# Hardware loops on ScalarE and VectorE in a batched A·Bᵀ kernel, with GpSimd passing on DMA landings as counts

## The chip, the cores and the metric

One core of one Trainium2 chip. The metric is the device time of one execution in microseconds (us). The span of a profile, from first to last instruction, is some 1.8 us shorter than the timed run (124.3 against 126.1 us for the profiled run of before). A run counts as slow when it is over 1.5% above the fastest of the same kernel. The granted clock is the share of TensorE's full clock that the profile records as granted.

## The reference

```python
a: (16, 512, 512) float32      # batch, m, k
b: (16, 512, 512) float32      # batch, n, k
out = np.matmul(a, b.transpose(0, 2, 1)).astype(np.float32)
```

33.55 MB are read and 16.78 MB written.

## The kernel before

Two batch entries form a pair; there are eight. Tiles of 2 MB are loaded into seven buffers. VectorE casts them to bf16 (first half of k into h, second half into w, later copied w to h). TensorE (PE) transposes them into PSUM; VectorE evicts (copies out of PSUM) the transposes of b into tb, ScalarE those of a into ta. PE multiplies, ScalarE evicts the products into one of seven output buffers. PE runs a hardware loop over pairs already; ScalarE and VectorE are unrolled. Their parts, cut:

```python
for u in range(pairs):                                  # VectorE, unrolled in Python
    for x, (h, w, s_c, s_t) in enumerate(both):         # both = a's and b's buffers
        n = 2 * u + x
        src = ld[n % NL]                                # a constant slot
        nc.vector.wait_ge(s_ld[n % NL], 16 * (n // NL + 1))    # the DMA's own semaphore
        ...                                             # n < 2: in two halves, as each lands
        nc.vector.tensor_copy(out=h[:], in_=src[:, :, :HK]).then_inc(s_c, 1)
        nc.vector.tensor_copy(out=w[:], in_=src[:, :, HK:]).then_inc(s_cd, 1)
    for ko in range(KO): ...                            # ha<-wa, tb0, hb<-wb, tb1, tb2, tb3

nc.scalar.nop().then_inc(s_ea, 2)
for u in range(pairs):                                  # ScalarE, unrolled in Python
    for ko in range(KO):
        nc.scalar.wait_ge(s_ta, KO * u + ko + 1)
        ...                                             # two copies ta<-tp
    for e in range(2):
        i = 2 * u + e
        ...                                             # wait for the store of i - NO
        for j in range(J):
            nc.scalar.wait_ge(s_mm, J * i + j + 1)
            ...                                         # copy ob[i % NO]<-ps[j]; s_pv or s_out
```

Of the kernel before, what the change touches and what calls it, by code (L numbers as in the profile page):

```python
# [10 lines left out]
def kernel(  # L11
# [6 lines left out]
    nc = tc.nc  # L18
    P = 128
    batch, M, K = a.shape  # L20
    _, N, _ = b.shape
    J = M // P
    KO = K // P
    HP = P // 2
    HK = K // 2
    pairs = batch // 2
    f32 = mybir.dt.float32
    bf16 = mybir.dt.bfloat16
    NL = 7
    NO = 7  # L30


    ORDER = "LLLLLLLSLLLLSLSSLSLSLLSSSSSSSSS"

    def sbuf(name, shape, dtype):
        return ctx.enter_context(nc.sbuf_tensor(name, shape, dtype))

    def sem(name):
        return tc.alloc_semaphore(name)

    with tc.tile_critical(no_gpsimd_drain=True):  # L41
        ident = sbuf("ident", [P, P], bf16)
        ld = [sbuf(f"ld{i}", [P, 2 * J, K], f32) for i in range(NL)]
        ha, wa, hb, wb = (
            sbuf(name, [P, 2 * J, HK], bf16) for name in ("ha", "wa", "hb", "wb")
        )
        ta = sbuf("ta", [P, KO, 2 * J * P], bf16)
        tb = sbuf("tb", [P, KO, 2 * J * P], bf16)
        ob = [sbuf(f"ob{i}", [P, J, N], f32) for i in range(NO)]
        tp = ctx.enter_context(nc.psum_tensor("tp", [P, 4, 2 * J, P], bf16))  # L50
        ps = ctx.enter_context(nc.psum_tensor("ps", [P, 4, N], f32))

# [1 line left out]
        s_ld = [sem(f"s_ld{i}") for i in range(NL)]  # L54
        s_second = [sem(f"s_second{i}") for i in range(2)]
        s_st = [sem(f"s_st{i}") for i in range(NO)]
        s_cd = sem("s_cd")
        s_ca = sem("s_ca")
        s_cb = sem("s_cb")
        s_ta = sem("s_ta")  # L60
        s_tb = sem("s_tb")
        s_ea = sem("s_ea")
        s_eb = sem("s_eb")
        s_mm = sem("s_mm")
        s_pv = sem("s_pv")
        s_out = sem("s_out")
# [5 lines left out]
            out=ident[:], in_=ident[:], compare_op=mybir.AluOpType.not_equal, fill=1.0,  # L72
# [4 lines left out]



        n_ld, n_st = 0, 1  # L80
        for what in ORDER:
            if what == "L":
                u, slot = n_ld // 2, n_ld % NL
                src = (a if n_ld % 2 == 0 else b)[2 * u:2 * u + 2].rearrange(
                    "e (p j) k -> (e p) j k", j=2 * J
                )
                if n_ld >= NL:

                    nc.sync.wait_ge(s_cd, n_ld - NL + 1)
                if n_ld < 2:  # L90
                    nc.sync.dma_start(
                        ld[slot][:, :J, :], src[:, :J, :]
                    ).then_inc(s_ld[slot], 16)
                    nc.sync.dma_start(
                        ld[slot][:, J:, :], src[:, J:, :]
                    ).then_inc(s_second[slot], 16)
                else:
                    nc.sync.dma_start(ld[slot][:], src).then_inc(s_ld[slot], 16)
                n_ld += 1
            else:  # L100
                slot = n_st % NO
                nc.sync.wait_ge(s_out, n_st + 1)
                nc.sync.dma_start(
                    out[n_st].rearrange("(p j) n -> p j n", j=J), ob[slot][:]
                ).then_inc(s_st[slot], 16)
                n_st += 1
        for n in range(batch - NO, batch - 1):
            nc.sync.wait_ge(s_st[n % NO], 16 * (n // NO + 1))




        nc.vector.nop().then_inc(s_eb, 2)
        nc.vector.wait_ge(s_set, 2)
        both = ((ha, wa, s_ca, s_ta), (hb, wb, s_cb, s_tb))
        for u in range(pairs):
            for x, (h, w, s_c, s_t) in enumerate(both):
                n = 2 * u + x
                src = ld[n % NL]
                nc.vector.wait_ge(s_ld[n % NL], 16 * (n // NL + 1))  # L120
                nc.vector.wait_ge(s_t, KO * u)
                if n >= 2:
                    nc.vector.tensor_copy(out=h[:], in_=src[:, :, :HK]).then_inc(s_c, 1)  # L123
                    nc.vector.tensor_copy(out=w[:], in_=src[:, :, HK:]).then_inc(s_cd, 1)  # L124
                else:
                    nc.vector.tensor_copy(out=h[:, :J, :], in_=src[:, :J, :HK])  # L126
                    nc.vector.tensor_copy(out=w[:, :J, :], in_=src[:, :J, HK:])  # L127
                    nc.vector.wait_ge(s_second[n], 16)
                    nc.vector.tensor_copy(  # L129
                        out=h[:, J:, :], in_=src[:, J:, :HK]  # L130
                    ).then_inc(s_c, 1)
                    nc.vector.tensor_copy(  # L132
                        out=w[:, J:, :], in_=src[:, J:, HK:]
                    ).then_inc(s_cd, 1)
            for ko in range(KO):
                if ko < 2:
                    h, w, s_c, s_t = both[ko]
                    nc.vector.wait_ge(s_cd, 2 * u + ko + 1)
                    nc.vector.wait_ge(s_t, KO * u + 2)
                    nc.vector.tensor_copy(out=h[:], in_=w[:]).then_inc(s_c, 1)  # L140
                nc.vector.wait_ge(s_tb, KO * u + ko + 1)
                nc.vector.tensor_copy(  # L142
                    out=tb[:, ko, :],
                    in_=tp[:, 2 + ko % 2].rearrange("k j p -> k (j p)"),
                ).then_inc(s_eb, 1)


        nc.scalar.nop().then_inc(s_ea, 2)
        for u in range(pairs):
            for ko in range(KO):  # L150

                nc.scalar.wait_ge(s_ta, KO * u + ko + 1)
                for e in range(2):
                    c = nc.scalar.copy(  # L154
                        out=ta[:, ko, e * J * P:(e + 1) * J * P].rearrange(
                            "k (j p h) -> k j p h", j=J, h=2
                        ),
                        in_=tp[:, ko % 2, :, e * HP:(e + 1) * HP].rearrange(
                            "k (h j) p -> k j p h", h=2
                        ),  # L160
                    )
                c.then_inc(s_ea, 1)
            for e in range(2):
                i = 2 * u + e
                if i >= NO:
                    nc.scalar.wait_ge(s_st[i % NO], 16 * (i // NO))
                for j in range(J):
                    nc.scalar.wait_ge(s_mm, J * i + j + 1)

                    c = nc.scalar.copy(  # L170
                        out=ob[i % NO][:, j, :].rearrange("m (p j) -> m p j", j=2 * J),
                        in_=ps[:, j, :].rearrange("m (j p) -> m p j", j=2 * J),
                    )
                    if j == J - 1:
                        c.then_inc(s_out, 1)
                    elif e == 0 or j == 0:
                        c.then_inc(s_pv, 1)
                    if i == 1 and j == 0:
                        nc.scalar.wait_ge(s_out, 1)
                        nc.scalar.dma_start(  # L180
                            out[0].rearrange("(p j) n -> p j n", j=J), ob[0][:]
                        ).then_inc(s_st[0], 16)


        def take(s, n):
            nc.tensor.wait_ge(s, n).then_inc(s, -n)  # L186

        pe = nc.tensor.engine
        with nc.Fori(0, pairs, engines=[pe]):
            with nc.Fori(0, 2, engines=[pe]):  # L190

                for x, (h, s_c, s_t, s_e) in enumerate(
                    ((ha, s_ca, s_ta, s_ea), (hb, s_cb, s_tb, s_eb))
                ):
                    take(s_c, 1)
                    for g in range(2):
                        take(s_e, 1)
                        for j in range(2 * J):
                            t = nc.tensor.transpose(  # L199
                                tp[:, 2 * x + g, j, :], h[:, j, g * P:(g + 1) * P], ident[:]  # L200
                            )
                        t.then_inc(s_t, 1)
            nc.tensor.wait_ge(s_ea, 2)
            nc.tensor.wait_ge(s_eb, 2)


            for e in range(2):
                for j in range(J):
                    if e == 1 and j % 2 == 0:
                        take(s_pv, 2)  # L210
                    for ko in range(KO):
                        t = nc.tensor.matmul(  # L212
                            ps[:, j, :],
                            ta[:, ko, (e * J + j) * P:(e * J + j + 1) * P],
                            tb[:, ko, :].rearrange("k (j p) -> k j p", j=2 * J)[
                                :, :, e * HP:(e + 1) * HP
                            ],
                            start=(ko == 0),
                            stop=(ko == KO - 1),
                        )  # L220
                    t.then_inc(s_mm, 1)
# [34 lines left out]
```

## Time and profile before

| | before |
|---|---|
| time, median of the first 3 runs | 127.23 us (127.03 to 127.98) |
| span of the profile | 124.3 us |
| DMA | 50.33 MB, engines over 90% busy in all slices but the ends |
| PE, VectorE, ScalarE busy | 74%, 55%, 57% |
| matmuls of one pair to those of the next | 12.40 to 12.46 us |
| last eviction done | 115.43 us |

### The profile page before, as it was taken

The numbers are of one execution on the slowest core, as the hardware profiler recorded it, in microseconds if no ns is written. First come the engines' busy times: TensorE is split into PE (matmuls) and PEld (weight loads), VectorE is DVE, ScalarE is ACT, GpSimd is POOL, SyncE is SP. The second block draws the span as 40 slices with busy tenths as digits, with TensorE's granted clock in tenths as the row PEclk, the third lists the DMA queues.
The fourth block names the chain that finished last, engine by engine and source line by source line (L and its number), as shares of the span: only waits on it lengthen the run. The fifth ranks groups of instructions, "written<-read, shape, count | busy, mean of one in ns | idle before, by whom it ended". The sixth has DMA issues, their size and how long they took to land. (4 is left out here: it accounts for less than half of the span.)

```text
span 124.3 us, 2076 instructions
## 1 busy us (share of the span) xinstructions
PE 91.8 (74%) x768; PEld 56.5 (45%) x768; DVE 67.9 (55%) x84; ACT 71.0 (57%) x129; POOL 0.7 (1%) x6
## 2 busy tenths in 40 slices
PE   0005397998699869986998699869986998699000
PEld 0005394447444744574447444744474447443000
DVE  0065668827891788278907890782686568400000
ACT  4006042769476946694669476947694769476100
POOL 2000000000000000000000000000000000000000
PEclk9999999999999999999999999999999999999955
DMA  3999999999999999999999999999999999999980
GB/s 79 403 427 451 443 427 427 427 427 374 411 427 424 445 432 443 424 422 430 414 430 406 416 451 387 403 451 416 448 427 422 419 422 427 427 427 427 424 377 34
DMA packets 4898, 50.35 MB, mean 405 GB/s; under 512 B 544, under 2 KB 544, under 8 KB 544
## 3 DMA queue, kind: packets, MB, share of 16 engines
q1 hardware_dynamic: 4752, 49.29, 94.5%
q10 hardware_dynamic: 144, 1.05, 2.0%
q14 instruction: 2, 0.02, 0.0%
HBM read 33.55 MB, written 16.78 MB: 405 GB/s over the span
## 5 line engine op out<-in xcount | busy, mean ns | idle before, releaser
L212 PE MATMUL ps<-tb,ta 128*128 128x512 bf16 x256 | 57.3, 379 | 8.0 <-DVE tb L142 8.0
L170 ACT COPY ob<-ps 128x512 f32<-128x512 f32 x64 | 37.6, 587 | 30.1 <-PE ps L212 30.1
L212 PEld LDWEIGHTS ps<-tb,ta 128*128 128x128 bf16 x256 | 23.9, 97 | 39.0 <-ACT ta L154 8.2
L154 ACT COPY ta<-tp 128x512 bf16<-128x512 bf16 x64 | 32.9, 604 | 13.3 <-PE tp L199 12.9
L199 PE MATMUL tp<-ident,ha 128*128 128x128 bf16 x256 | 19.7, 230 | 11.8 <-PEq L186 10.9
L199 PEld LDWEIGHTS tp<-ident,ha 128*128 128x128 bf16 x256 | 16.7, 104 | 15.5 <-issue 13.8
L142 DVE COPY tb<-tp 128x1024 bf16<-128x1024 bf16 x32 | 21.3, 685 | 3.9 <-PE tp L199 3.6
L199 PE MATMUL tp<-ident,hb 128*128 128x128 bf16 x256 | 18.5, 230 | 3.1 <-PEq L186 3.1
L199 PEld LDWEIGHTS tp<-ident,hb 128*128 128x128 bf16 x256 | 16.3, 104 | 3.4 <-issue 3.3
L140 DVE COPY ha<-wa 128x2048 bf16<-128x2048 bf16 x8 | 5.5, 693 | 18.1 <-PE tp L199 18.1
L123 DVE CAST hb<-ld 128x2048 bf16<-128x2048 f32 x7 | 8.6, 1226 | 7.2 <-DMA ld<-in_b_dram 7.2
L123 DVE CAST ha<-ld 128x2048 bf16<-128x2048 f32 x7 | 8.5, 1219 | 0.6 <-DMA ld<-in_a_dram 0.6
L124 DVE CAST wb<-ld 128x2048 bf16<-128x2048 f32 x7 | 8.5, 1221 | 0.0
L124 DVE CAST wa<-ld 128x2048 bf16<-128x2048 f32 x7 | 8.5, 1220 | 0.0
L140 DVE COPY hb<-wb 128x2048 bf16<-128x2048 bf16 x8 | 5.5, 685 | 0.2 <-PE tp L199 0.2
L126 DVE CAST ha<-ld 128x1024 bf16<-128x1024 f32 x1 | 0.7, 694 | 6.1 <-DMA ld<-in_a_dram 6.1
L154 ACT ACT_TABLE_LOAD x1 | 1.3, 1283 | 1.0 <-SPq L41 1.0
L129 DVE CAST hb<-ld 128x1024 bf16<-128x1024 f32 x1 | 0.7, 694 | 1.2 <-DMA ld<-in_b_dram 1.2
L126 DVE CAST hb<-ld 128x1024 bf16<-128x1024 f32 x1 | 0.7, 695 | 1.2 <-DMA ld<-in_b_dram 1.2
L129 DVE CAST ha<-ld 128x1024 bf16<-128x1024 f32 x1 | 0.7, 694 | 1.1 <-DMA ld<-in_a_dram 1.1
L132 DVE CAST wa<-ld 128x1024 bf16<-128x1024 f32 x1 | 0.7, 689 | 0.0
L127 DVE CAST wa<-ld 128x1024 bf16<-128x1024 f32 x1 | 0.7, 687 | 0.0
(8 smaller groups left out, 2.3 us busy)
## 6 DMA issues: line engine op xcount, KB each, us to landing
out_dram<-ob SPq DMA_DIRECT2D x15, 1024.0 KB, 25.8
ld<-in_a_dram SPq DMA_DIRECT2D x7, 2048.0 KB, 30.8
ld<-in_b_dram SPq DMA_DIRECT2D x7, 2048.0 KB, 30.5
ld<-in_a_dram SPq DMA_DIRECT2D x2, 1024.0 KB, 6.1
ld<-in_b_dram SPq DMA_DIRECT2D x2, 1024.0 KB, 10.1
out_dram<-ob ACTq DMA_DIRECT2D x1, 1024.0 KB, 12.2
```

The source lines that it names most:

```text
L123: nc.vector.tensor_copy(out=h[:], in_=src[:, :, :HK]).then_inc(s_c, 1)
L124: nc.vector.tensor_copy(out=w[:], in_=src[:, :, HK:]).then_inc(s_cd, 1)
L126: nc.vector.tensor_copy(out=h[:, :J, :], in_=src[:, :J, :HK])
L127: nc.vector.tensor_copy(out=w[:, :J, :], in_=src[:, :J, HK:])
L129: nc.vector.tensor_copy(out=h[:, J:, :], in_=src[:, J:, :HK]).then_inc(s_c, 1)
L132: nc.vector.tensor_copy(out=w[:, J:, :], in_=src[:, J:, HK:]).then_inc(s_cd, 1)
L140: nc.vector.tensor_copy(out=h[:], in_=w[:]).then_inc(s_c, 1)
L142: nc.vector.tensor_copy(out=tb[:, ko, :], in_=tp[:, 2 + ko % 2].rearrange("k j p -> k (j p)"),).then_inc(s_eb, 1)
L154: c = nc.scalar.copy(out=ta[:, ko, e * J * P:(e + 1) * J * P].rearrange("k (j p h) -> k j p h", j=J, h=2), in_=tp[:, ko % 2, :, e * HP:(e ...
L170: c = nc.scalar.copy(out=ob[i % NO][:, j, :].rearrange("m (p j) -> m p j", j=2 * J), in_=ps[:, j, :].rearrange("m (j p) -> m p j", j=2 * J),)
L199: t = nc.tensor.transpose(tp[:, 2 * x + g, j, :], h[:, j, g * P:(g + 1) * P], ident[:])
L212: t = nc.tensor.matmul(ps[:, j, :], ta[:, ko, (e * J + j) * P:(e * J + j + 1) * P], tb[:, ko, :].rearrange("k (j p) -> k j p", j=2 * J)[:, ...
```

## The change

The intent: less program. ScalarE and VectorE run one turn of a hardware loop per pair, with buffer slots held in registers. The waits of a loop body are written once, with one count and one semaphore for all turns, so each wait takes its counts back ("take": wait, then subtract), and GpSimd turns the DMAs' semaphores into one count for loads (s_go) and one for freed output buffers (s_of). All stores go out from the SyncE queue. Cut to its core:

```diff
-    ORDER = "LLLLLLLSLLLLSLSSLSLSLLSSSSSSSSS"
+    ORDER = "LLLLLLLSSLLLLSLSSLSLSLLSSSSSSSSS"
...
-                    nc.sync.wait_ge(s_cd, n_ld - NL + 1)
+                    nc.sync.wait_ge(s_cd, n_ld - NL + 2)
...
+                nc.gpsimd.wait_ge(s_ld[n_ld % NL], 16 * (n_ld // NL + 1)).then_inc(s_go, 1)
...
+        def taker(engine):
+            return lambda s, n: engine.wait_ge(s, n).then_inc(s, -n)
...
-        for u in range(pairs):
+        with nc.Fori(0, pairs, engines=[dve]) as u:
...
+                src = ld[:, bass.ds((u * 2 + x) % NL, 1)].rearrange("p o j k -> p (o j) k")
+                take(s_go, 1)
+                nc.vector.tensor_copy(out=h[:], in_=src[:, :, :HK]).then_inc(s_c, 1)
+                ...                                # w in two halves, s_cd on the first
...
         nc.scalar.nop().then_inc(s_ea, 2)
+        nc.scalar.nop().then_inc(s_of, NO)
-        for u in range(pairs):
+        with nc.Fori(0, pairs, engines=[act]) as u:
...
+            take(s_of, 2)
             for e in range(2):
+                dst = ob[:, bass.ds((u * 2 + e) % NO, 1)].rearrange("m o j n -> m (o j) n")
...
-                    if i == 1 and j == 0:          # the store of out 0 from ScalarE's queue
-                        ...
...
+                            if x == 1 and g == 0 and j == 0:     # PE: ha has been read
+                                t.then_inc(s_da, 1)
```

## The prediction

The forecast came to 127.1 us, with a range of 126.4 to 129.0.

- *The first pair and the second bound:* the time that GpSimd takes to pass a landing on, the author's estimate. The +0.8 us of the first pair contain it.
- *The slack:* the time from a DMA's issue to its first bytes. The average end of the transfers, the 118.5 us as the latest end of compute and so the "about 3 us" were worked out with it, as estimates. What before shows is 1.0 us (first load issued at 0.94 us, first packet at 1.95 us).
- *Rivals B and C*, with chances of 0.05 and 0.02: back edges that wait for an instruction fetch, and casts that get slower when their slot comes from a register.

Three measured facts of before: by the packets, the slowest of the 16 DMA engines was done at 122.5 us; the one store on ScalarE's queue took 2.0% of engine time for 1.05 MB, as much per MB as the SyncE queue's 94.5% for 49.29 MB; and the casts of 128x2048 took 1219 to 1226 ns, which the prediction assumed for the loop too.

> **What bounds the kernel now.** I read the page's slices first, then the table of stages, then the chain of waits, then the issues of the SyncE queue.
>
> ```profile
> DMA  3999999999999999999999999999999999999980
> ...
> HBM read 33.55 MB, written 16.78 MB: 405 GB/s over the span
> ...
> out_dram<-ob SPq DMA_DIRECT2D x15, 1024.0 KB, 25.8
> ld<-in_a_dram SPq DMA_DIRECT2D x7, 2048.0 KB, 30.8
> ```
>
> All slices but the first and the last have the DMA engines at 9 tenths or more, and a transfer takes 25 to 31 us from issue to landing although 1 MB at the slices' usual 427 GB/s needs only 2.5 us: it stands in a backlog. 50.33 MB / 427 GB/s = 117.9 us[...]. The span is 124.3 us. So DMA bandwidth sets the time, and compute matters only if it lets the backlog run dry.
>
> How near is compute to that? The table of stages, one stage per pair, start of matmuls to start of matmuls:
>
> ```profile
> core 0: us, PE busy (x) PEld busy (x) DVE busy (x) ACT busy (x) POOL busy (x), PEclk, DMA share, GB/s
> 32.90:45.30 12.40, 11.04 (x96) 6.69 (x96) 8.41 (x11) 8.71 (x16) 0.00 (x0) 1.00 1.00 426
> ...
> 82.70:95.10 12.40, 11.10 (x96) 6.67 (x96) 8.28 (x10) 8.70 (x16) 0.00 (x0) 1.00 1.01 429
> ```
>
> A pair moves 6.29 MB, 14.7 us of DMA, but computes in 12.4 us. The first seven loads give compute a start, and it meets the loads again only at pairs 6 and 7 (VectorE waits 3.3 and 2.5 us for their second tile). PE sets the 12.4: about 7.0 us of matmuls and 5.4 us of transposes, in which PE, VectorE and ScalarE hand over to each other. The end of the kernel:
>
> ```profile
> 114.84 0.59 ACT L170 COPY ob<-ps 128x512 f32<-128x512 f32 x1 [0.28 <-PE ps L212]
> ...
> 118.00:119.00 1.00, 0.00 (x0) 0.00 (x0) 0.00 (x0) 0.00 (x0) 0.00 (x0) 0.77 1.01 426
> ...
> 120.00:121.00 1.00, 0.00 (x0) 0.00 (x0) 0.00 (x0) 0.00 (x0) 0.00 (x0) 0.50 0.78 328
> 121.00:122.00 1.00, 0.00 (x0) 0.00 (x0) 0.00 (x0) 0.00 (x0) 0.00 (x0) 0.50 0.33 139
> ```
>
> Compute ends at 115.4 us, the last store is issued at 115.5 and lands 7.6 us later. Its own 1.05 MB need 2.5 us, so the slowest engine, done at 122.5, starts on it at about 120.0.[...] **Compute has about 3 us of slack at the end.** The question is whether the change delays its last step by more than that.
>
> [...] Here PE's two loops show 76 ns not taken and 208 ns taken, plus a 36 ns ALU operation; I use these. [...] the page has two instruction packets in all, in mid-kernel, with no stall visible.[...]
>
> **The change, part by part.**
>
> *First pair.* Each of the first two tiles is now cast only after both halves land. Before, the first halves were cast early: ha half at 6.11, second half at 8.52, ready at 9.21; hb second half at 13.49, ready at 14.18. After: [...]the whole h cast of 1.22 us. [...]then the two w halves (0.69 each, started 0.61 apart) until 16.1. The copy ha<-wa, at 14.70 before, comes at about 16.0. The second transposes of ha, at 16.14 before, move to about 16.95; the next hand-overs absorb nothing. **About +0.8 us, once.**
>
> *Each later pair: VectorE.* One instruction more per tile: w in two halves, 2 x 0.61 against 1.13 us of issue distance, +0.1 us per tile; register arithmetic for the slot (some 5 operations at PE's spacing of 0.1 us) and one back edge, below 1 us in all. It lies beside the matmuls, where VectorE has 3 us to spare:
>
> ```profile
> 28.72 0.69 DVE L140 COPY ha<-wa 128x2048 bf16<-128x2048 bf16 x1 [3.07 <-PE tp L199]
> ...
> 31.56 1.29 DVE L142 COPY tb<-tp 128x1024 bf16<-128x1024 bf16 x2 [0.34 <-PE tp L199]
> ...
> 28.24 4.17 ACT L154 COPY ta<-tp 128x512 bf16<-128x512 bf16 x8
> ```
>
> On the path are only waits that end last. ha<-wa is released by the first transpose of hb in place of the last of ha, 56 ns later by PE's spacing; the third tb copy had its wait folded in and now has a separate wait-and-subtract, about 65 ns (the gap from the 21 ns wait of L139 to its copy). Other turns wait for the engine, not the semaphore. About +0.1 us per pair.
>
> *ScalarE.* Slot arithmetic falls into the 1.7 us before its first eviction and into the 0.28 us gaps, where PE is ahead at 0.86 us per tile against 0.59. The back edge lies between the last eviction and the first ta copy, back to back today: 0.25 us, mostly under the 0.48 us that the eviction holds the engine. The ta copies end 0.45 us before VectorE's last tb copy, so at most 0.1 us shows.
>
> So 0.1 to 0.2 us per pair, on seven pairs 0.7 to 1.4 us. With the first pair: **compute ends 1.5 to 2.2 us later, at 117 to 117.6 us, inside the 118.5.** A second bound, the last tile's landing at 100.4[...], is no later.
>
> *Loads.* The count that frees a slot comes one tile later (s_cd is now a first half). The fourth refill, issued at 30.44, now waits for the next pair's first tile, some 35.5 us. It had 26 us of backlog ahead of it, so nothing moves. The other late loads stand behind stores, which wait longer (99.9 us of SyncE's waits are for ScalarE's evictions).
>
> *The store of out 0* joins the one queue. The 27 to 30 us stretch, where it shared the engines with a load, ran at 382 GB/s against 427: 0.13 MB, 0.3 us, which may come back.
>
> *Stores as counts*: ScalarE waits for both output slots of a pair at once. With the backlog's order (2.47 us per MB), the latest, store 8, lands near 105, and pair 7's first eviction is at 108.7. No wait.
>
> Sum: 0 from compute, up to -0.3 from the store: **127.1 us.**
>
> **Rivals.** *A: compute becomes the bound.* If loop overhead puts 0.7 us or more per pair on the path, the last store goes out after 0.8 + 4.9 = 5.7 us, 2.7 past the slack: slower by 2%. For it: register-addressed instructions have no row here, and both engines lie on PE's 5.4 us hand-over. Against: PE's own loops cost it 0.2 us per turn. [...] *D: faster*, through something outside the span (126.1 against 124.3 us)[...]. I see no 2.5 us there.
>
> **Range and chances.** The three runs of before spread over 0.95 us. Slack swallowed gives 126.6 to 127.6; A in part gives up to 129. I take 126.4 to 129.0. Faster 0.03; slower 0.12 (A 0.05, B 0.05, C 0.02); the rest within 2%.
>
> **What would show it.** Right: DMA slices stay at 9 to the end; pair to pair 12.5 to 12.6 us; first pair's matmuls at about 21.4 us (20.59 before); last eviction at 116.5 to 117.8; casts still 1.22 us; the last store lands in about 5.5 us in place of 7.6. Wrong: a DMA slice below 9 before the last two; pair to pair above 13.1 us; ScalarE idle before its first ta copy of a pair; many more instruction packets[...].

## More of the kernel before

PE waits before the matmuls of (e=1, j=2) for two counts of s_pv; the last of them is the eviction of (e=1, j=0).

```profile
L154 ACT ACT_TABLE_LOAD x1 | 1.3, 1283 | 1.0 <-SPq L41 1.0
```

It says that ScalarE loads its activation table once, for 1.28 us, at the start (0.98 us), where it costs nothing: ScalarE waits 8.3 us more for its first transposes.

## The result, and the profile after

The changed kernel is **slower**: ratio 1.1029 (95% interval 1.0954 to 1.1103). A ratio is the mean time of one kernel's fast runs over that of the other's fast runs of the same rounds, so not quite the ratio of quoted medians. Of its four runs two were fast (140.44 and 140.62 us) and two slow (151.40 and 151.54 us, with a mean granted clock of 0.861 against 0.947); before had no slow run. The range of the prediction ended at 129.0.

From the page of after (a fast run), the slices of PE, the clock and DMA, then two groups:

```profile
span 138.8 us, 2355 instructions
...
PE   0005569966897689867995699479986699579920
...
PEclk9999999999999999999999999955999999956998
DMA  4999999999999999999999999999999946600364
...
L151 DVE CAST ha<-ld 128x2048 bf16 x8 | 9.8, 1221 | 9.1 <-DVEq L132 9.0
...
L185 ACT ACT_TABLE_LOAD x8 | 10.3, 1283 | 1.3 <-SPq L41 1.2
```

DMA is full until slice 32 and then starves: compute has become the bound. The clock falls to half (0.50) in two places, from 90.2 and from 120.9 us, for 6.8 us each. And the table load is there eight times. The casts with a slot from a register still take 1.22 us, so rival C is out. The page has no instruction packets (before had two, at 50.1 and 58.7 us), and the trace has the taken back edges at 45 ns (ScalarE) and 56 ns (VectorE), so rival B is out.

Where the load stands is seen in ScalarE's timeline between two pairs (start, duration, what, and in brackets the idle time before it):

```profile
42.55 0.59 ACT L203 COPY ob<-ps 128x512 f32 x1 [0.35 <-ACTq L132]
43.16 1.28 ACT L185 ACT_TABLE_LOAD   x1
44.45 2.05 ACT L185 COPY ta<-tp 128x512 bf16<-128x512 bf16 x4
```

The last eviction of a pair and the first ta copy of the next stood 0.48 us apart before (27.76 to 28.24 us). Now it is 1.90 us, in each of the seven turns: 1.42 us more, at a place where PE's next transposes wait for the ta copies (PE stands idle 1.53 us there, against 0.20 us before). Two stages of after, the second at half clock in part:

```profile
core 0: us, PE busy (x) PEld busy (x) DVE busy (x) ACT busy (x) POOL busy (x), PEclk, DMA share, GB/s
35.10:49.30 14.20, 11.12 (x97) 6.68 (x98) 8.46 (x13) 9.98 (x17) 0.00 (x0) 1.00 0.99 387
...
92.10:108.70 16.60, 13.51 (x96) 7.23 (x96) 8.62 (x13) 9.98 (x17) 0.00 (x0) 0.85 0.99 422
```

A pair takes 14.2 us in place of 12.4, and 16.6 where the clock halves. ScalarE's busy time per pair rose from 8.7 to 10.0 us, far below the 14.2, so it is not a bound by its busy time.

### The profile page after: what moved, and what is told of

The parts are those of the page before. It is cut to its first block, busy times and chain, and to the rows that moved or that the text cites. A ratio compares the mean times of both kernels' runs of the same rounds, so it can differ in the third digit from the quotient of the medians.

```text
span 138.8 us, 2355 instructions
## 1 busy us (share of the span) xinstructions
PE 96.9 (70%) x768; PEld 57.3 (41%) x768; DVE 68.3 (49%) x96; ACT 79.9 (58%) x136; POOL 0.7 (1%) x6
## 5 line engine op out<-in xcount | busy, mean ns | idle before, releaser
L240 PE MATMUL ps<-tb,ta 128*128 128x512 bf16 x256 | 62.3, 399 | 9.2 <-DVE tb L167 8.8
L203 ACT COPY ob<-ps 128x512 f32 x64 | 37.5, 585 | 38.6 <-PE ps L240 32.9
L240 PEld LDWEIGHTS ps<-tb,ta 128*128 128x128 bf16 x256 | 24.9, 101 | 44.1 <-issue 12.6
L185 ACT COPY ta<-tp 128x512 bf16<-128x512 bf16 x64 | 32.2, 608 | 13.8 <-PE tp L225 13.7
L225 PEld LDWEIGHTS tp<-ident,hb 128*128 128x128 bf16 x256 | 16.6, 105 | 3.2 <-issue 3.2
L151 DVE CAST ha<-ld 128x2048 bf16 x8 | 9.8, 1221 | 9.1 <-DVEq L132 9.0
L151 DVE CAST hb<-ld 128x2048 bf16 x8 | 9.8, 1222 | 3.0 <-DVEq L132 3.0
L185 ACT ACT_TABLE_LOAD x8 | 10.3, 1283 | 1.3 <-SPq L41 1.2
L155 DVE CAST wb<-ld 128x1024 bf16 x8 | 5.5, 687 | 0.0
L152 DVE CAST wb<-ld 128x1024 bf16 x8 | 5.5, 687 | 0.0
L155 DVE CAST wa<-ld 128x1024 bf16 x8 | 5.5, 687 | 0.0
L152 DVE CAST wa<-ld 128x1024 bf16 x8 | 5.5, 686 | 0.0
## 6 DMA issues: line engine op xcount, KB each, us to landing
ld<-in_b_dram SPq DMA_DIRECT2D x7, 2048.0 KB, 28.8
ld<-in_b_dram SPq DMA_DIRECT2D x2, 1024.0 KB, 10.2
```

The source lines that it names most:

```text
L152: nc.vector.tensor_copy(out=w[:, :J, :], in_=src[:, :J, HK:]).then_inc(s_cd, 1)
L155: nc.vector.tensor_copy(out=w[:, J:, :], in_=src[:, J:, HK:]).then_inc(s_w, 1)
L185: c = nc.scalar.copy(out=ta[:, ko, e * J * P:(e + 1) * J * P].rearrange("k (j p h) -> k j p h", j=J, h=2), in_=tp[:, ko % 2, :, e * HP:(e ...
L203: c = nc.scalar.copy(out=dst[:, j, :].rearrange("m (p j) -> m p j", j=2 * J), in_=ps[:, j, :].rearrange("m (j p) -> m p j", j=2 * J),)
L225: t = nc.tensor.transpose(tp[:, 2 * x + g, j, :], h[:, j, g * P:(g + 1) * P], ident[:])
L240: t = nc.tensor.matmul(ps[:, j, :], ta[:, ko, (e * J + j) * P:(e * J + j + 1) * P], tb[:, ko, :].rearrange("k (j p) -> k j p", j=2 * J)[:, ...
```

## The experiments

Theory 1: the table load in each turn, on the hand-over from evictions to ta copies, is the main cost. Rival 2: the loop's own work (register operations, separate waits, back edge) is. Theory 3: what is left over is PE's clock, which halves because the longer hand-over leaves PE idle. Seven kernels ran, all with correct results; the first four share a chip and the runs of before, and so do the last three.

### 1. A copy ahead of the loop

The guess behind this run is that the compiler places the load by what it knows at that point of the program. In after, no activation stands before the loop, so on entry no table would be known to be loaded, and the load would land in the body. One tiny copy ahead of the loop should then move it out:

```diff
+        warm = sbuf("warm", [P, 1], bf16)
...
         nc.scalar.nop().then_inc(s_ea, 2)
+        nc.scalar.wait_ge(s_set, 2)
+        nc.scalar.copy(out=warm[:], in_=ident[:, :1])
         nc.scalar.nop().then_inc(s_of, NO)
         with nc.Fori(0, pairs, engines=[act]) as u:
```

> The changed kernel with one 128x1 ScalarE copy ahead of its loop, so that the activation table is already known to be loaded when the loop starts. Theory 1 (the table load in each turn, 1.28 us busy and 1.42 us between the last eviction and the first ta copy): one table load in place of eight, matmuls to matmuls 12.7 to 12.8 us in place of 14.2, last eviction near 118, 127 to 128.5 us. Rival (register operations, back edge and separate waits on the hand-over): the loads go but the pairs stay above 13.5 us, and the time above 133 us.

Measured: 127.53 us (126.77 to 127.95, 4 runs), ratio 1.0033 (0.9976 to 1.0091), the same as before. The trace has one load, at the line of the new copy ahead of the loop, and none in it. ScalarE's timeline between two pairs:

```profile
42.02 0.59 ACT L206 COPY ob<-ps 128x512 f32 x1 [0.35 <-ACTq L133]
42.50 4.11 ACT L188 COPY ta<-tp 128x512 bf16<-128x512 bf16 x8
```

The group of its table loads on the page, one execution, and then two stages of the table by pairs:

```profile
L178 ACT ACT_TABLE_LOAD x1 | 1.3, 1283 | 1.0 <-SPq L41 1.0
```

```profile
34.55:47.35 12.80, 11.12 (x97) 6.67 (x98) 8.47 (x13) 8.69 (x16) 0.00 (x0) 1.00 1.00 383
47.35:60.14 12.79, 11.12 (x97) 6.66 (x97) 8.55 (x13) 8.69 (x16) 0.00 (x0) 1.00 1.01 430
```

The 0.48 us between eviction and ta copy are back, with loop, register slots and takes all still there. A pair takes 12.80 us: 1.40 less than after, 0.40 more than before. The loss in time, as far as it can be measured, goes with that one copy. That it takes the load out of the loop is shown; how the compiler decides is not. Rival 2 falls as the main cause; its 0.40 us per pair are real.

### 2 and 3. The load without the loop: on the path, and beside it

In the kernel before, unrolled, a 128x1 activation in each of pairs 1 to 7, Exp and Sqrt in turn, brings seven more loads of 1283 ns, one ahead of each activation. In one kernel they stand ahead of the ta copies, in the other between ta copies and evictions, where ScalarE waits for the first matmuls anyway (1.6 to 1.7 us in before). The core of the edit (the buffer cold, its memset and the waits for it are cut):

```diff
...
+            if u > 0:
+                nc.scalar.activation(
+                    out=cold[:, 1:2], in_=cold[:, 0:1],
+                    func=(mybir.ActivationFunctionType.Exp, mybir.ActivationFunctionType.Sqrt)[u % 2],
+                )
...
```

> The kernel before, unrolled, with a table load forced ahead of the ta copies of pairs 1 to 7 by a 128x1 activation of another table set (Exp and Sqrt in turn). Theory 1: about 1.3 us of load and 0.2 to 0.3 us of activation on the path, matmuls to matmuls about 14.0 us, compute ends near 127 us, 130 to 140 us in all by what the PE clock does. Rival (loop overhead): no loop here, so below 129 us.

> The same seven table loads and activations, but after the ta copies, where ScalarE waits some 1.6 us for the first matmuls. Theory 1 with the load counting only where it stands on the hand-over: matmuls to matmuls 12.4 to 12.6 us, 126.8 to 128 us. If a table load costs wherever it stands (ScalarE as a bound by its busy time): the time of the run with the load on the path.

Measured: on the path 140.61 us, 0.6 us above the expected range, ratio 1.1085 (1.1022 to 1.1147; one of four runs slow, at 142.85); beside it 126.83 us, ratio 0.9993 (0.9939 to 1.0047). ScalarE's timeline of the kernel with the load on the path:

```profile
43.99 0.59 ACT L178 COPY ob<-ps 128x512 f32<-128x512 f32 x1 [0.28 <-PE ps L220]
44.59 1.28 ACT L154 ACT_TABLE_LOAD   x1
45.89 0.20 ACT L154 ACTIVATE cold<-cold 128x1 f32<-128x1 f32 x1
45.99 0.57 ACT L162 COPY ta<-tp 128x512 bf16<-128x512 bf16 x1
```

The same of the kernel with the load beside the path:

```profile
40.10 4.17 ACT L157 COPY ta<-tp 128x512 bf16<-128x512 bf16 x8
44.29 1.28 ACT L167 ACT_TABLE_LOAD   x1
45.59 0.20 ACT L167 ACTIVATE cold<-cold 128x1 f32<-128x1 f32 x1
45.92 0.59 ACT L178 COPY ob<-ps 128x512 f32<-128x512 f32 x1
```

And one stage of each at whole clock, in the same order:

```profile
81.20:95.13 13.93, 11.08 (x97) 6.68 (x98) 8.32 (x11) 10.07 (x18) 0.00 (x0) 1.00 1.02 434
```

```profile
32.46:44.86 12.40, 11.04 (x96) 6.69 (x97) 8.41 (x11) 10.18 (x19) 0.00 (x0) 1.00 1.03 429
```

Same loads, nearly the same busy time of ScalarE (10.1 and 10.2 us per pair), 13.9 against 12.4 us. On the path, last eviction and first ta copy stand 2.01 us apart in place of 0.48, and the pair grows by the same 1.5 us. A load at that place, with no loop on ScalarE, is enough for a loss of the size of the whole change; moved behind the eight ta copies, it costs nothing that shows. Its price depends on where it stands. That the two times agree so closely (140.6 and 140.5 us) is partly chance: here no loop work is on the path, but the clock fell in three places and not in two (mean 0.924 against 0.948).

### 4. PE kept busy

15 dummy 128x128 matmuls (0.84 us at the 56 ns from start to start of the transposes; PE's idle time there fell from 1.53 to 0.69 us) at the end of each inner turn of the transposes, into a PSUM bank that is free there:

```diff
                         t.then_inc(s_t, 1)
+                for _ in range(15):
+                    nc.tensor.matmul(
+                        ps[:, 0, :P], ident[:], ident[:], start=True, stop=True
+                    )
             nc.tensor.wait_ge(s_ea, 2)
```

> The changed kernel with 15 dummy 128x128 matmuls at the end of each inner turn of the transposes, into a PSUM bank that is free there, shorter than the waits that they fill. Theory 3 (PE's clock halves because the longer hand-over leaves PE idle): granted clock 1.0 until the matmuls end, every pair at 14.2 us, compute ends near 128.5, 132.5 to 135 us, no run near 151 us. If the halved clock has another cause: clock and times as of the changed kernel, 140 to 151 us.

Measured: 136.50 us (136.06 to 137.18, 4 runs), ratio 1.0749 (1.0694 to 1.0803), no run near 151. This misses the expected 132.5 to 135 by 1.5 us: the matmuls of the first pair began at 22.7 us, not 20.9 as in after, and compute ended at 130.2. The clock in the page's slices, then one late stage:

```profile
PEclk9999999999999999999999999999999999999996
```

```profile
107.90:122.10 14.20, 12.80 (x126) 8.36 (x127) 8.33 (x12) 9.98 (x17) 0.00 (x0) 1.00 0.62 260
```

More work on PE, and a faster kernel than after: the clock stays whole to the end of the matmuls and each pair takes 14.2 us. So the halved clock comes from PE's low activity: with the dummies PE is busy for 12.80 us of a pair's 14.20, in after for 11.12. This kernel is 4.0 us faster than after although its first pair is 1.8 us later; the sum below puts the cost of the clock in after at 5.3 us (3.2 and 2.1).

### 5. VectorE's loop alone

ScalarE's code unrolled again as before (constant slots, one table load); VectorE's loop and GpSimd's passing on of loads kept. The diff is the inverse of the ScalarE part of the change.

> The changed kernel with ScalarE's code unrolled again as before (constant slots, waits folded into the copies, one table load), VectorE's loop and the passing on of loads kept. If the 0.40 us per pair that stayed with the copy ahead of the loop are ScalarE's register operations and separate waits: matmuls to transposes 6.97 us again (7.11 there), pairs at 12.4 to 12.5 us, 126.5 to 127.5 us. If they are VectorE's: pairs at 12.6 to 12.8 us, last eviction at 117 or later, 126.5 to 127.8 us.

Measured: 127.54 us (127.14 to 128.14), ratio 1.0062 (1.0010 to 1.0115), within 2%. A stage takes 12.6 us:

```profile
34.10:46.70 12.60, 11.14 (x96) 6.68 (x97) 8.45 (x13) 8.71 (x16) 0.00 (x0) 1.00 1.00 390
```

This splits the 0.40 us per pair that stayed in experiment 1. From the first matmul of a pair to the next transpose it is 6.97 us before and here, 7.11 in after and copy_first: 0.14 us are ScalarE's. From that transpose to the next matmuls it is 5.43 us before, 5.64 here, 5.69 in copy_first: 0.21 are VectorE's. The last 0.05 us, between 5.64 and 5.69, appear only with both loops. Neither of the two expectations held alone.

### 6. The first store on the SyncE queue alone

The kernel before with only the store of out 0 moved, as in the change: the new ORDER, and ScalarE's dma_start taken out.

> The kernel before with the first store on the SyncE queue as in the change, nothing else. My prediction's step: the 27 to 30 us stretch at 382 GB/s is two queues sharing the engines, and some 0.3 us come back (ratio 0.997 to 0.998). Rival: the dip is stores and loads mixing and stays whatever the queue: ratio 1.000 within the interval, and a stretch below 400 GB/s still there when the first stores run.

Measured: 127.14 us (126.77 to 128.07, 6 runs), ratio 1.0029 (0.9985 to 1.0073). Nothing comes back. The stretches of this kernel:

```profile
27.00:30.00 3.00, 2.75 (x42) 2.31 (x40) 1.65 (x3) 2.67 (x7) 0.00 (x0) 1.00 1.01 431
35.00:38.00 3.00, 3.00 (x15) 1.30 (x14) 2.02 (x2) 1.90 (x5) 0.00 (x0) 1.00 0.98 311
```

The dip left the 27 to 30 us stretch, and a deeper one stands at 35 to 38, where one queue alone runs: the second queue is not its cause. Nor is it simply stores mixing with loads. By this trace's packets, load packets that start between 35.0 and 37.4 us take up to 1.4 us in place of 0.61, and the first store's packets start only at 37.5. In before, load packets take up to 0.92 us between 27.5 and 29.0, and the first store's start at 28.8. In both, slow load packets come ahead of the first store; why stays open.

### 7. The changed kernel again

The question is whether the second group of after's times (151 us at a mean granted clock of 0.861) is theory 3 in more pairs, or a disturbance from outside.

> The changed kernel as it is, for more runs of it. [...]runs fall into few groups, each time going with its clock, the slower the lower: near 140.5 us at 0.947, near 151.5 at 0.861, perhaps some between, and the span differs by about 2.4 us for each pair whose matmuls run at half clock. If it is a disturbance from outside, the kernel before in the same rounds shows it too.

Measured: six runs, one fast (140.62 us, clock 0.948), five slow (146.95 at 0.902, 149.04 at 0.880, 149.38 at 0.881, 151.51 at 0.861, 151.80 at 0.850). Before, in the same rounds, had none slow: 126.28 to 127.32. This time the profile fell on one (151.51), and it shows what they are. The page's slices, then one stage:

```profile
span 149.7 us, 2355 instructions
...
PEclk9999999995699659995699758999998579965999
```

```profile
36.50:53.00 16.50, 13.62 (x96) 7.81 (x96) 8.56 (x13) 10.06 (x17) 0.00 (x0) 0.81 0.98 402
```

It is theory 3 in more pairs: six of the seven stages took 15.2 to 16.6 us, the other 14.8, against 14.2 at whole clock. By and large the times go with the clock, but not in the few groups that were expected, and why one run falls to half clock in two mid-kernel places and another in six is not shown. The eviction-to-copy distance is 1.90 us as in the fast run. Against slow runs as an outside disturbance speak before in the same rounds and pe_filler, which had none in four.

## Why the prediction was wrong

**The step that failed** is in the part on ScalarE. It listed what the loop adds between the last eviction and the first ta copy: "The back edge lies between the last eviction and the first ta copy, back to back today: 0.25 us, mostly under the 0.48 us that the eviction holds the engine." The list left out the table load, which this loop body has, and which it does not have where a copy stands before it (copy_first). Back edge and the rest do hide: copy_first has the 0.48 us of before. The load added 1.42 us there.

The next step failed with it: "The ta copies end 0.45 us before VectorE's last tb copy, so at most 0.1 us shows." That took the 0.45 us as slack, yet 1.40 of the 1.42 us came out in each pair: the late ta copies hold back PE's second transposes (PE idle 1.53 us ahead of them, 0.20 in the kernel before), and these the third tb copy (VectorE idle 1.90 us, 0.34 in the kernel before). And the prediction had no term at all for PE's clock, which took 5.3 us more.

The sum, from the traces of fast runs (last eviction done at 133.62 against 115.43 us, +18.2):

| term | predicted | measured |
|---|---|---|
| first pair | +0.8 | +0.3 |
| table load, seven turns | 0 | 7 x 1.40 = +9.8 |
| loop work on the path, seven turns | +0.7 to 1.4 | 7 x 0.40, less 0.2 for four stages of before at 12.46, = +2.6 |
| half clock in mid-kernel (stages of 14.45, 16.59, 14.75 us against 14.20) | 0 | +3.2 |
| last pair, first matmul to last eviction (10.13 against 7.81 us) | 0 | +2.3, some 2.1 of it clock (pe_filler: 8.06) |
| compute ends later by | +1.5 to 2.2 | +18.2 |
| less DMA time behind the last eviction (8.9 us to the end of the span before, 5.2 after) | all of it | -3.7 |
| span | about 0 | +14.5 (138.8 - 124.3) |

The small +0.3 of the first pair looks like luck with the clock, which was whole from 18.5 us on in after and from 19.6 in before (the first sixteen transposes took 1.86 us in both, those at 18.69 us in after 1.06). In copy_first and dve_loop, whole from 20.7 and 19.9 us, the first matmuls began 1.2 and 0.9 us later than before's. One cost in this term was too small: between a landing and its cast the prediction had GpSimd's passing on alone. In after it is 0.44 and 0.33 us (8.56 to 9.00, 13.53 to 13.86 us), against 0.03 before: VectorE's takes and the slot's register operation (118 and 124 ns) come on top.

**Right:** what bounds the kernel, and the slack. The prediction let compute end as late as about 118.5 us. (Its time from issue to first bytes was too long: the first packet starts 1.0 us after the first load's issue in before, and 0.8 us after the last store's in after. With 1.0 us, an end of compute at 115.4 and the slowest engine's start on the last store at 120.0, the slack was nearer 3.6 us, an estimate from these figures.)

| kernel | last eviction done, us | span, us |
|---|---|---|
| before | 115.4 | 124.3 |
| dve_loop | 117.8 | 125.7 |
| copy_first | 119.4 | 126.2 |
| pe_filler | 130.2 | 135.4 |
| after | 133.6 | 138.8 |

Before's span in the rounds of the experiments was 124.5 to 125.6 us. Up to 119.4 the span follows by less than half; from copy_first to pe_filler 10.8 us of compute bring 9.2 us of span. Rival A's threshold (0.7 us per pair on the path) is not contradicted: 0.40 us per pair left the time within 2%, 1.8 us did not; nothing between was run. It had a chance of 0.05, and it happened, from a source that the rival did not name. Rivals B and C didn't happen.

**Right in kind, wrong in size:** the loop's work. ScalarE's register operations were to vanish in waits, and cost 0.14 us. The trace shows why: each eviction now starts with a register operation (46 to 117 ns), which in six of the eight of a pair carries the wait for the matmul. The first of a pair runs it 1.06 us after the pair's first matmul, where before's copy began, and the copy follows at 1.20; PE waits for the eviction of (e=1, j=0). VectorE's +0.1 is 0.21: in dve_loop ha<-wa comes 1.26 us after the first transpose against 1.16 before, and the third tb copy 4.20 against 4.00. How much of this is the separate take and how much the changed release, the runs don't separate.

**Right, and idle:** the fourth refill was issued at 36.7 us (35.5 predicted) and SyncE waited 6.0 us for it, without a gap in DMA there. **Wrong, and small:** the 0.3 us of the first store; the dip is not the second queue's.

**Left open:** a version that beats both was not found. copy_first and before stand at the limit of DMA (at 9 tenths or more in all slices but the ends), where less work on an engine shows little: 0.40 us per pair less gave a ratio of 1.0033 (0.9976 to 1.0091).

## What to carry to other kernels

When code moves into a loop, ask what the compiler may have placed in the body, the activation table load above all: look in the trace for a load that comes once per turn, and put one activation ahead of the loop (eight loads became one here). Price an added instruction by where it stands: 1.28 us of table load cost nothing beside PE's matmuls (load_beside, ratio 0.9993) and, between eviction and transposes, together with the clock that fell after it and the loop's own work, turned a kernel with some 3.6 us of slack (the estimate above) into one 10% slower. And when a hand-over grows, check the granted clock: here PE's idle time in it grew from 0.20 to 1.53 us, and in two of after's pairs the matmuls that followed ran in part at a clock of 0.50.

## Single costs in these traces

- The table load takes 1283 ns. In after the first ta copy started 1.29 us after the load's start, and 1.42 us is all that the load added. Where Exp and Sqrt alternate (load_on_path), the load starts as the eviction ends (44.57 and 44.59 us) and the activation 1.30 us later. With no activation ahead of the loop the load came eight times, with one copy ahead it came once.
- PE's clock: in after the longest idle time of PE in a hand-over was 1.53 us by the profile, the same in all seven, and the clock fell after two of them. The clock's recorded stretches in after, whole and half in turn, last 71.68, 6.83, 23.89, 6.83 and 10.24 us, which is 21, 2, 7, 2 and 3 times 3.413 us; the one of before 98.99 us, 29 times. An estimate from these two traces, with stretches of 3.41 us laid on the clock's own transitions: PE was busy for 1.53 and 1.51 us in the two ahead of the falls in mid-kernel, for nothing in the two ahead of the falls after the last matmul, and for 1.70 us or more in the other 56, none of which was followed by half clock. The line was drawn after the fact and is untested. The stretch before the first fall in after, and the first half of the time at half clock that follows:

```profile
86.70:90.10 3.40, 1.50 (x25) 1.34 (x25) 1.85 (x4) 3.39 (x8) 0.00 (x0) 1.00 0.98 414
90.10:93.50 3.40, 2.41 (x16) 1.34 (x14) 2.83 (x4) 0.97 (x2) 0.00 (x0) 0.51 1.01 431
```

- A taken compare-and-branch took 208 ns on PE, 45 on ScalarE and 56 on VectorE (after, the loops' own lines).
- A register-held slot on a copy: its register operation took 46 to 117 ns on ScalarE and, where it carries a wait, runs behind it. The copy itself was no slower (585 against 587 ns).
